# Score products of a two-map attention: full-array products of stacked hi and lo against products of 64 rows in two row tiles

## The chip, the cores and the metric

The kernel runs on one core of one Trainium2 chip. The metric is the device time of one execution in microseconds (us). Three timed runs of the kernel before took 1775.22, 1769.58 and 1770.94 us; the median is 1770.94 us.

## The reference, cut to what matters

The program is a two-layer backbone over 256 context tokens and 256 latent tokens of width 1024. Each layer normalises its input and feeds three mixers: a state-space scan (branch A), a differential attention (branch B) and a matrix-memory recurrence (branch C). Their outputs are gated, projected, merged and projected once more. Only branch B is touched here. It has 8 heads, each with two softmax maps over a head dimension of 64:

```python
def diff_attend(qb, k_all, v_all, lam):
    s = jnp.einsum('bqhcd,bkhcd->bhcqk', qb, k_all)       # c: the two maps, d: 64
    p = jax.nn.softmax(s, axis=-1)
    a = p[:, :, 0] - lam * p[:, :, 1]
    return jnp.einsum('bhqk,bkhe->bqhe', a, v_all)
```

Context queries see the 256 context keys; latent queries see all 512 keys. Layer 0 needs the outputs of all 512 tokens, layer 1 those of the 256 latent tokens alone.

## The kernel before, in words

There are four token tiles of 128 tokens (`NT` = 4): tiles 0 and 1 are context, 2 and 3 latent. `tq` holds the tiles whose outputs are needed, four in layer 0 and two (2 and 3) in layer 1. A quarter `qt` of the channels holds two heads; `qkv_proj(qt)` projects q, k and v of two heads in token layout, and `attn_prep(qt)` normalises and rotates q and k.

Products that must keep float32 accuracy are made of two operands in a reduced format (float32r): `hi`, the rounded value, and `lo`, the rest. A projection is then three products, hi x hi, hi x lo and lo x hi. They are the lines 149 to 151 (128 x 256 at a time) and 180 to 182 (mostly 128 x 512), and their weights are split on chip after each load (lines 119 to 121: ScalarE casts, VectorE subtracts).

`attn_tr(qt, h)` brings q and k of one head into channel layout with transposes on TensorE (lines 911 and 920): the 128 channels of a head are two maps of 64 rows each, in partitions 0 to 63 and 64 to 127. For each map it then builds, on 64 partitions at a time, one tile with hi of q in the map's own rows and lo of q in the other rows (lines 914 to 917), one tile with hi of k in both halves (lines 924 to 926; the second half is a copy made by GpSimd), and lo of k in the map's own rows (line 927).

`attn_head(qt, h)` goes over the token tiles `t` of `tq`. For each it makes the scores of both maps, 128 queries by N keys, with N = 256 for t < 2 and N = 512 otherwise. A map takes two matmuls: line 948 uses all 128 rows (hi x hi and lo x hi in one pass) and line 949 the 64 rows of the map (hi x lo). Each map has its own PSUM bank (`pe()`, three buffers). Then follow the row maximum (VectorE, line 951), the exponential (ScalarE, line 953), the difference of the two maps (VectorE, line 960), its transposes on TensorE (line 963), a copy (line 965) and the product with v (line 967). The group of four score matmuls of one tile `t` is called a set below. There are 48 sets: in layer 0, 8 heads with two sets of N = 256 and two of N = 512; in layer 1, 8 heads with two sets of N = 512.

The order on each engine is fixed when the program is built. A planner simulates the program and picks, for each engine, the ready instruction with the best priority; `band(0)` (loads, splits, evacuations) goes ahead of `band(1)` (the mixers), and that ahead of `band(2)` (projections). So projections that are due anyway (`fill`, lines 1025 to 1031, and those queued before) stand between the steps of the attention. After the attention comes branch C, in layer 0 together with `mod_block` (line 266), which computes modulation columns on VectorE, ScalarE and GpSimd.

Of the kernel before, what the change touches and what calls it, by code (L numbers as in the profile page):

```python
# [9 lines left out]
F32 = mybir.dt.float32  # L10
# [24 lines left out]
def hybrid_backbone_kernel(ctx: ExitStack, tc: tile.TileContext, A, out, dbg=None):  # L35
# [4 lines left out]
    # ---- priority bands: 0 loads, splits and evacuations; 1 mixers; 2 projections  # L40
# [52 lines left out]
    def bc(ap, n):  # L93
        """append a broadcast free dim of n"""
        return ap.unsqueeze(len(ap.shape)).to_broadcast(list(ap.shape) + [n])

    # ---- constants
# [20 lines left out]
    # ---- weight stream: granules of 4 k-tiles by 256 columns; hi/lo split on chip  # L118
# [4 lines left out]
    def granules(srcs):  # L123
        """srcs: dram pieces [1024, n] that make 256 columns; yields (k0, hi, lo)"""
        for g in range(2):
            with band(0):
                raw = mk(wts, [P, 4, 256], "raw", bufs=3)
                c = 0
                for src in srcs:
                    n = src.shape[1]  # L130
                    nc.sync.dma_start(
                        raw[:, :, c : c + n],
                        src[g * 512 : (g + 1) * 512, :].rearrange("(k p) n -> p k n", p=P),
                    )
                    c += n
                hi = mk(wts, [P, 4, 256], "whi", F32R, bufs=3)
                lo = mk(wts, [P, 4, 256], "wlo", F32R, bufs=3)
                split(raw, hi, lo)
            yield 4 * g, hi, lo

    def mm_tok(ps, lhs, tcol, k0, hi, lo):
        """one pair of token tiles times 4 k-tiles of weights; both tiles share a bank"""
        xh, xl = lhs
        for i in range(2):
            sl = slice(tcol + i * P, tcol + (i + 1) * P)
            o = ps[:, i * 256 : (i + 1) * 256]
            for j in range(4):
                k = k0 + j
                T.matmul(o, lhsT=xh[:, k, sl], rhs=hi[:, j, :], start=(k == 0 and i == 0), stop=False)  # L149
                T.matmul(o, lhsT=xh[:, k, sl], rhs=lo[:, j, :], start=False, stop=False)  # L150
                T.matmul(o, lhsT=xl[:, k, sl], rhs=hi[:, j, :], start=False, stop=(k == KT - 1 and i == 1))  # L151

    def proj_tok(srcs, lhs, pairs, evac):
        """out[tok, 256]; a pair of token tiles per bank, evacuated as [128, 2, 256]"""
        ps = {}
        with band(2):
            for p in pairs:
                ps[p] = pacc()
        for k0, hi, lo in granules(srcs):
            with band(2):  # L160
                for p in pairs:
                    mm_tok(ps[p], lhs, p * 256, k0, hi, lo)
        for p in pairs:
            with band(0):
                evac(p, ps[p].rearrange("p (t n) -> p t n", t=2))

    def proj_ch(srcs, lhs, ranges, evac, halves=False, gr=None):
        """out[128 channels, tokens] for 2 channel tiles; ranges[i] = (tok0, tok1)"""
# [34 lines left out]
    def rsqrt(src, n, scale, eps, pp=P, pool_=True):  # L203
        """1/sqrt(src*scale+eps) for a narrow [pp, n] tile"""
# [18 lines left out]
    # ---- modulation columns of one layer: four column tiles of the array share the contraction  # L223
    def mod_pair(l, cbs, pool, bufs, rbufs, between=None, each=None, end=False):
        with band(2):
            ps = pacc()
            for x, cb in enumerate(cbs):
                if x and between:
                    between()
                for k0 in range(0, KT, 2):  # L230
# [10 lines left out]
                    for j in range(2):  # L241
                        k = k0 + j
                        g = k % 4
                        # the second block's rows lie two below the first's
# [21 lines left out]
    def mod_block(l, cb, pool):  # L266
        """512 columns of the modulation: multiplied and added up by k-tile, TensorE sums the partitions"""
# [41 lines left out]
    # ---- narrow parameters of a layer: loads, and what is made of them  # L309
    def narrow(l, pool):  # L310
# [7 lines left out]
        gcs = mk(small, [P, 2, 2, 64], "gcs", bufs=1)  # (q|k), lat tile: cos * gain  # L318
        gsn = mk(small, [P, 2, 2, 64], "gsn", bufs=1)  # (q|k), lat tile: signed sin * swapped gain
# [16 lines left out]
        def compute():  # L336
            # scaled sign and decay columns
# [3 lines left out]
            # -lambda  # L341
# [5 lines left out]
            # rotary tables with the gains folded in; 1/sqrt(64) goes into q  # L347
# [11 lines left out]
    # ================= set-up  # L359
# [4 lines left out]
    with band(0):  # L364
# [11 lines left out]
        # small loads go between the large ones  # L376
        few = []
        for l in range(depth):
            w_ = prow[l]
            # per-channel parameters as rows: 16 for each layer  # L380
# [22 lines left out]
        # silu of the conditioning vectors, as columns  # L403
# [14 lines left out]
    def columns(l):  # L418
# [5 lines left out]
        # convolutions feed silu(x) = (x/2)(1 + tanh(x/2)): taps and bias are halved  # L424
# [8 lines left out]
    # the first weights, ahead of the second half of the modulation  # L433
# [17 lines left out]
    xcur = None  # x of the latent tiles after layer 0  # L451

    class Tokens:
        """token-layout [tokens, 1024] in slots of [128, 2 tiles, 512 columns]"""
# [4 lines left out]
        def __call__(self, b, p):  # L459
            """block of 256 columns of a pair of tiles: [128, 2, 256]"""  # L460
            return self.t[b // 2, p][:, :, (b % 2) * 256 : (b % 2 + 1) * 256]

        def tile(self, g, t):
            """half of the columns of one token tile: [128, 512]"""
            return self.t[g, t // 2][:, t % 2, :]

        def col(self, t, k):
            """[128 tokens, 128 channels]"""
            return self.tile(k // 4, t)[:, (k % 4) * P : (k % 4 + 1) * P]

    for l in range(depth):
        last = l == depth - 1
        w_in = A["w_in"][l]
        pq = (1,) if last else (0, 1)  # pairs of token tiles whose outputs are needed
# [13 lines left out]
        # ================= modulated norm -> hT (hi, lo)  # L488
# [63 lines left out]
        # ---------- pools of this layer  # L552
# [5 lines left out]
        sm = mk(mlrow, [P, 512], "sm", F32R)  # -M rows, hi over lo  # L558
        mlc = mk(mlrow, [P, 5, NT, 8], "mlc")  # w, sc, em, wk, cdec columns
        sa = mk(sp, [P, 512], "sa", F32R)  # L560
        col = mk(sp, [P, 5, NT, 2, 16], "col")  # -acs, exp(acs), dt*exp(end-acs), dt, exp(end)
# [19 lines left out]
        with band(1):  # L581
# [61 lines left out]
            # rows -> columns  # L643
# [8 lines left out]
            # per-chunk scalars on all partitions  # L652
# [32 lines left out]
        # ---------- depthwise convolution + silu of a channel tile (in PSUM) -> [128, n]  # L685
# [13 lines left out]
        # gate path: 2 silu(z) of [128, 2, 256]  # L699
# [7 lines left out]
        # ================= branch A: SSD  # L707
# [34 lines left out]
        def ssd_core(g):  # L742
            hs = slice(8 * g, 8 * g + 8)
            with band(1):
# [10 lines left out]
                # chunk states  # L755
# [70 lines left out]
        # ================= branch B: q, k, v of two heads  # L826
# [43 lines left out]
        # ================= branch B: differential attention  # L870
# [31 lines left out]
        halves_ = (slice(0, 64), slice(64, 128))  # the two maps of a head  # L902

        def attn_tr(qt, h):
            """q as hi over lo (map 1: lo over hi), k as hi over hi, and the lo of k"""
            res = qkv[qt][0]
            with band(1):
                q2, k2 = [], []
                pt = pm()
                for t in tq:  # L910
                    T.transpose(chunk(pt, t), res["q"][:, t, h * P : (h + 1) * P], ident)
                for m in range(2):
                    own, oth = halves_[m], halves_[1 - m]
                    x = mk(ap, [P, 512], f"q{m}", F32R, bufs=2)
                    S.copy(x[own, lo_:], pt[own, lo_:])
                    tt(x[oth, lo_:], pt[own, lo_:], x[own, lo_:].bitcast(F32), ALU.subtract)
                    q2.append(x)
                pt = pm()
                for t in range(NT):
                    T.transpose(chunk(pt, t), res["k"][:, t, h * P : (h + 1) * P], ident)  # L920
                kl = mk(ap, [P, 512], "kl", F32R, bufs=2)
                for m in range(2):
                    own, oth = halves_[m], halves_[1 - m]
                    x = mk(ap, [P, 512], f"k{m}", F32R, bufs=2)
                    S.copy(x[own], pt[own])
                    tsc(x[oth], x[own].bitcast(F32), 1.0, ALU.mult, 0.0, ALU.add, eng=G)
                    tt(kl[own], pt[own], x[own].bitcast(F32), ALU.subtract)
                    k2.append(x)
            aS[qt, h] = q2, k2, kl

        def attn_head(qt, h):
            vt = qkv[qt][0]["v"]
            ssB, r0B = aS[qt]
            q2, k2, kl = aS[qt, h]
            with band(1):
                po = pm()
                for t in tq:
# [8 lines left out]
                    for m in range(2):  # L946
                        o, own = es[m][0], halves_[m]
                        T.matmul(o, lhsT=q2[m][:, qs], rhs=k2[m][:, 0:N], start=True, stop=False)  # L948
                        T.matmul(o, lhsT=q2[m][own, qs], rhs=kl[own, 0:N], start=False, stop=True)  # L949
# [4 lines left out]
                    # E0 - lambda (sum0 / sum1) E1; the factor 1 / sum0 joins the norm below  # L954
# [20 lines left out]
        def attn_fin(qt):  # L975
            ssB, r0B = aS[qt]
            with band(1):
                # rms over a head: r0 / sqrt(mean((r0 o)^2) + eps)
# [19 lines left out]
        # ================= branch C: projections of one mLSTM head  # L998
# [49 lines left out]
        # branch A: rms over the row  # L1048
# [16 lines left out]
        # ================= branch C: mLSTM  # L1065
# [75 lines left out]
        def mo_post(j, ths):  # L1141
            with band(1):
# [8 lines left out]
                # zz holds 2 silu(z)  # L1151
# [74 lines left out]
        # ================= merge, in channel layout  # L1226
# [4 lines left out]
        per = D // nqt  # channel tiles in a slot of mixed  # L1231
        per = 2 if nqt == 512 else 4

        def transposed(y, scale_of):
            """token layout -> (hi, lo) [128, 8, tokens], scaled by a per-channel column"""
# [47 lines left out]
        # ================= output projection and residual  # L1283
        ep = tc.alloc_tile_pool(name=f"out{l}", bufs=1)
        xnew = Tokens(yx, "y", pq) if not last else xcur
        with band(1):
            gbc = {}
            for p in pq:
                gbc[p] = mk(ep, [P, D], "gbc", bufs=2)
                cc = 1 - p  # L1290
                for hf in range(2):
# [3 lines left out]
                    # half of the gate: the merge gates are 1 + tanh  # L1295
# [41 lines left out]
        # the other half of the columns: weights resident, one pair of token tiles after the other  # L1337
# [79 lines left out]
```

## Time and profile before

| What | Value |
|---|---|
| Median of three runs | 1770.94 us |
| Lowest and highest run | 1769.58 and 1775.22 us |
| Span of the profiled execution, first to last instruction | 1772.7 us |
| Time of the profiled execution outside of its span | not listed apart from the span |
| TensorE busy (matmul) | 1707.9 us, 96% |
| VectorE busy | 1233.4 us, 70% |
| ScalarE busy | 829.6 us, 47% |
| GpSimd busy | 296.4 us, 17% |
| DMA, mean over the span | 102 GB/s |

The busy time of a matmul in the profile runs from its start to a modelled end, and neighbours overlap; what a matmul occupies is read from the distance between the starts of two neighbours. Attention of layer 0 lies from about 280 to 560 us of the span, that of layer 1 from about 1317 to 1482 us. PE is TensorE's matmul row, PEld its weight load, DVE VectorE, ACT ScalarE, POOL GpSimd.

### The profile page before, as it was taken

To read this page: it belongs to the slowest core of one execution; us is meant where nothing else is said; L and a number is where in the kernel's file an instruction comes from. 1 tells how busy PE (TensorE), PEld (TensorE's weight loads), DVE (VectorE), ACT (ScalarE), POOL (GpSimd) and SP (SyncE) were. 2 spreads that over 40 slices of the span, in tenths; PEclk is the share of its full clock that TensorE was granted. 3 is DMA by queue.
4 is the path that set the end of the run, shared out by engine and by line. 5 is a ranking of instruction groups with operands and counts; after the bars stand their busy time and mean duration, and the time that the engine had idled before them with its cause. 6 is when DMAs were issued, how large, how long until landed. Compare 5 with 4: busy or idle time off the path is not lost.

```text
span 1772.7 us, 28884 instructions
## 1 busy us (share of the span) xinstructions
PE 1707.9 (96%) x11256; PEld 1512.4 (85%) x11256; DVE 1233.4 (70%) x2279; ACT 829.6 (47%) x1609; POOL 296.4 (17%) x296
## 2 busy tenths in 40 slices
PE   5999999999999798899999999999999999999998
PEld 1787889999899687888888889888898989999998
DVE  4798887777765999973434445787887876776565
ACT  3455535554545465642323333545554555444453
POOL 1012331111000646520011000111221210000000
PEclk8999999999999898999999999999999999999999
DMA  8422112222223434423323334232232223335554
GB/s 257 120 72 65 55 60 72 62 70 61 74 60 107 132 119 143 143 62 96 96 83 95 96 119 112 67 89 84 72 120 72 84 78 114 95 97 171 177 176 143
DMA packets 192052, 180.39 MB, mean 102 GB/s; under 512 B 20750, under 2 KB 178064, under 8 KB 191916
## 3 DMA queue, kind: packets, MB, share of 16 engines
q1 hardware_dynamic: 191916, 178.54, 33.5%
q8 instruction: 89, 1.46, 0.3%
q14 instruction: 47, 0.39, 0.1%
HBM read 177.47 MB, written 1.05 MB: 101 GB/s over the span
## 4 chain that ended last, share of the span: by engine, by line
PE 55%; DVE 6%; issue 1%; ACT 1%; POOL 0%; DVEq 0%; POOLq 0%; ACTq 0%
PE acc L180 9%; PE acc L182 9%; PE acc L181 9%; PE acc L151 6%; PE acc L149 6%; PE acc L150 6%; DVE macc L79 1%; PE pm L967 1%; PE pe L949 1%; DVE dn L82 1%; PE pm L1120 1%; DVE wlo L82 1%; PE pe L948 1%; PE pm L764 1%; PE pe L1104 1%
## 5 line engine op out<-in xcount | busy, mean ns | idle before, releaser
L82 DVE TENSOR_TENSOR wlo<-raw,whi 128x1024 fp32r<-128x1024 f32 x274 | 349.5, 1276 | 263.1 <-ACT whi L120 261.5
L149 PE MATMUL acc<-whi,hh 128*128 128x256 f32 x1728 | 504.9, 292 | 7.8 <-DVE modc L82 5.1
L151 PE MATMUL acc<-whi,hl 128*128 128x256 f32 x1728 | 506.5, 293 | 0.0
L150 PE MATMUL acc<-wlo,hh 128*128 128x256 f32 x1728 | 506.3, 293 | 0.0
L120 ACT CAST whi<-raw 128x1024 fp32r<-128x1024 f32 x274 | 287.7, 1051 | 372.2 <-PE acc L181 238.4
L149 PEld LDWEIGHTS acc<-whi,hh 128*128 128x128 f32 x1728 | 333.6, 193 | 17.4 <-issue 5.7
L151 PEld LDWEIGHTS acc<-whi,hl 128*128 128x128 f32 x1728 | 333.6, 193 | 10.7 <-issue 8.8
L150 PEld LDWEIGHTS acc<-wlo,hh 128*128 128x128 f32 x1728 | 333.6, 193 | 10.6 <-issue 8.1
L180 PE MATMUL acc<-hh,whi 128*128 128x512 f32 (+1 forms) x712 | 255.2, 361 | 2.5 <-DVE zz L79 2.5
L181 PE MATMUL acc<-hl,whi 128*128 128x512 f32 (+1 forms) x712 | 254.4, 358 | 0.2 <-DVE hl L82 0.2
L182 PE MATMUL acc<-hh,wlo 128*128 128x512 f32 (+1 forms) x712 | 253.3, 357 | 0.0
L180 PEld LDWEIGHTS acc<-hh,whi 128*128 128x128 f32 x712 | 134.4, 190 | 22.6 <-DVE zz L79 2.9
L181 PEld LDWEIGHTS acc<-hl,whi 128*128 128x128 f32 x712 | 135.0, 190 | 20.4 <-issue 3.1
L182 PEld LDWEIGHTS acc<-hh,wlo 128*128 128x128 f32 x712 | 135.0, 190 | 19.0 <-issue 1.2
L181 PE MATMUL acc<-yl,whi 128*128 128x512 f32 (+1 forms) x384 | 129.4, 339 | 0.0
L180 PE MATMUL acc<-yh,whi 128*128 128x512 f32 (+1 forms) x384 | 129.2, 339 | 0.0
L182 PE MATMUL acc<-yh,wlo 128*128 128x512 f32 (+1 forms) x384 | 128.9, 338 | 0.0
L82 POOL TENSOR_TENSOR macc<-macc,wm 128x512 f32<-128x512 f32 x56 | 81.3, 1452 | 116.6 <-ACT wm L290 106.4
L951 DVE TENSOR_REDUCE nmax<-pe 128x1 f32<-128x512 f32 (+1 forms) x96 | 56.3, 598 | 34.9 <-PE pe L949 33.7
L181 PEld LDWEIGHTS acc<-yl,whi 128*128 128x128 f32 x384 | 72.1, 188 | 8.5
L182 PEld LDWEIGHTS acc<-yh,wlo 128*128 128x128 f32 x384 | 71.9, 188 | 8.6
L180 PEld LDWEIGHTS acc<-yh,whi 128*128 128x128 f32 x384 | 72.0, 188 | 8.4
(310 smaller groups left out, 2848.8 us busy)
## 6 DMA issues: line engine op xcount, KB each, us to landing
raw<-in_w_in_dram SPq DMA_DIRECT2D x192, 512.0 KB
raw<-in_w_branch_dram SPq DMA_DIRECT2D x48, 512.0 KB
wm<-in_w_mod_dram SPq DMA_DIRECT2D x45, 512.0 KB
raw<-in_w_in_dram SPq DMA_DIRECT2D x48, 256.0 KB
raw<-in_w_out_dram SPq DMA_DIRECT2D x16, 512.0 KB
raw<-in_w_mod_dram SPq DMA_DIRECT2D x3, 512.0 KB
xin<-in_ctx_dram SPq DMA_DIRECT2D x2, 512.0 KB
xin<-in_x_dram SPq DMA_DIRECT2D x2, 512.0 KB
```

The costliest lines, as they stand in the source:

```text
L79: (eng or V).scalar_tensor_tensor(out=o, in0=a, scalar=s, in1=b, op0=op0, op1=op1)
L82: (eng or V).tensor_tensor(out=o, in0=a, in1=b, op=op)
L120: S.copy(hi, raw)
L149: T.matmul(o, lhsT=xh[:, k, sl], rhs=hi[:, j, :], start=(k == 0 and i == 0), stop=False)
L150: T.matmul(o, lhsT=xh[:, k, sl], rhs=lo[:, j, :], start=False, stop=False)
L151: T.matmul(o, lhsT=xl[:, k, sl], rhs=hi[:, j, :], start=False, stop=(k == KT - 1 and i == 1))
L180: T.matmul(o, lhsT=hi[:, j, cs], rhs=xh[:, k, a:b], start=(k == 0 and first), stop=False)
L181: T.matmul(o, lhsT=hi[:, j, cs], rhs=xl[:, k, a:b], start=False, stop=False)
L182: T.matmul(o, lhsT=lo[:, j, cs], rhs=xh[:, k, a:b], start=False, stop=(k == KT - 1 and final))
L764: T.matmul(pt, lhsT=BT[:, c, :], rhs=xw, start=True, stop=True)
L948: T.matmul(o, lhsT=q2[m][:, qs], rhs=k2[m][:, 0:N], start=True, stop=False)
L951: V.tensor_reduce(out=ng[:, m : m + 1], in_=es[m][0], axis=AX.X, op=ALU.max, negate=True)
```

## The change

`attn_tr` keeps q and k in their natural layout, both maps below each other in 128 partitions: one tile of hi and one of lo for q, and the same for k. Each is made by one ScalarE cast and one VectorE subtraction on 128 partitions. The tiles of swapped halves and the GpSimd copies go. `attn_head` makes the scores of a map by three matmuls of 64 rows (hi x hi, lo x hi, hi x lo); map 0 uses rows 0 to 63 of the array and map 1 rows 64 to 127, and the six matmuls of a set alternate between the two maps. The rest of the diff removes comments and docstrings.

```diff
         def attn_tr(qt, h):
             res = qkv[qt][0]
             with band(1):
-                q2, k2 = [], []
-                pt = pm()
-                for t in tq:
-                    T.transpose(chunk(pt, t), res["q"][:, t, h * P : (h + 1) * P], ident)
-                for m in range(2):
-                    own, oth = halves_[m], halves_[1 - m]
-                    x = mk(ap, [P, 512], f"q{m}", F32R, bufs=2)
-                    S.copy(x[own, lo_:], pt[own, lo_:])
-                    tt(x[oth, lo_:], pt[own, lo_:], x[own, lo_:].bitcast(F32), ALU.subtract)
-                    q2.append(x)
-                pt = pm()
-                for t in range(NT):
-                    T.transpose(chunk(pt, t), res["k"][:, t, h * P : (h + 1) * P], ident)
-                kl = mk(ap, [P, 512], "kl", F32R, bufs=2)
-                for m in range(2):
-                    own, oth = halves_[m], halves_[1 - m]
-                    x = mk(ap, [P, 512], f"k{m}", F32R, bufs=2)
-                    S.copy(x[own], pt[own])
-                    tsc(x[oth], x[own].bitcast(F32), 1.0, ALU.mult, 0.0, ALU.add, eng=G)
-                    tt(kl[own], pt[own], x[own].bitcast(F32), ALU.subtract)
-                    k2.append(x)
-            aS[qt, h] = q2, k2, kl
+                out = []
+                for nm_, ts, f0 in (("q", tq, lo_), ("k", range(NT), 0)):
+                    pt = pm()
+                    for t in ts:
+                        T.transpose(chunk(pt, t), res[nm_][:, t, h * P : (h + 1) * P], ident)
+                    xh = mk(ap, [P, 512], nm_ + "h", F32R, bufs=2)
+                    xl = mk(ap, [P, 512], nm_ + "l", F32R, bufs=2)
+                    S.copy(xh[:, f0:], pt[:, f0:])
+                    tt(xl[:, f0:], pt[:, f0:], xh[:, f0:].bitcast(F32), ALU.subtract)
+                    out += [xh, xl]
+            aS[qt, h] = out
...
-                    for m in range(2):
-                        o, own = es[m][0], halves_[m]
-                        T.matmul(o, lhsT=q2[m][:, qs], rhs=k2[m][:, 0:N], start=True, stop=False)
-                        T.matmul(o, lhsT=q2[m][own, qs], rhs=kl[own, 0:N], start=False, stop=True)
+                    for n, (x, y) in enumerate(((qh, kh), (ql, kh), (qh, kl))):
+                        for m in range(2):
+                            own = halves_[m]
+                            T.matmul(es[m][0], lhsT=x[own, qs], rhs=y[own, 0:N], start=(n == 0), stop=(n == 2))
```

## Rows read from the trace of the kernel before

**Rows 1.** The page: its first line, and TensorE's matmul row of part 1.

```profile
span 1772.7 us, 28884 instructions
...
PE 1707.9 (96%) x11256; PEld 1512.4 (85%) x11256; DVE 1233.4 (70%) x2279; ACT 829.6 (47%) x1609; POOL 296.4 (17%) x296
```

**Rows 2.** Stretches: length, busy us (instructions) by engine, PEclk, DMA share, GB/s.

```profile
280.00:560.00 280.00, 280.00 (x2014) 251.92 (x2013) 195.31 (x435) 143.10 (x312) 28.79 (x33) 1.00 0.23 66
1317.00:1482.00 165.00, 162.97 (x1142) 143.99 (x1142) 122.58 (x237) 90.27 (x175) 28.38 (x35) 0.98 0.27 79
...
575.00:765.00 190.00, 160.64 (x1015) 145.98 (x1014) 180.71 (x327) 106.66 (x209) 110.38 (x80) 0.92 0.43 130
...
1350.00:1360.00 10.00, 7.97 (x42) 6.44 (x42) 7.78 (x13) 4.86 (x10) 2.00 (x3) 0.74 0.36 105
```

**Rows 3.** PE in order of time (start, length, line), a set of N = 512.

```profile
489.77 0.60 PE L963 MATMUL pe<-ident,E 128*128 128x128 f32 x4
490.12 0.48 PE L948 MATMUL pe<-k,q 128*128 128x512 f32 x1
490.53 0.49 PE L949 MATMUL pe<-kl,q 64*128 64x512 f32 x1
...
491.39 0.50 PE L949 MATMUL pe<-kl,q 64*128 64x512 f32 x1
491.82 0.38 PE L151 MATMUL acc<-whi,hl 128*128 128x256 f32 x1
492.04 0.28 PE L149 MATMUL acc<-whi,hh 128*128 128x256 f32 x1
492.16 0.28 PE L150 MATMUL acc<-wlo,hh 128*128 128x256 f32 x1
```

**Rows 4.** PE in order of time, projection matmuls of 512 columns.

```profile
477.70 0.39 PE L182 MATMUL acc<-hh,wlo 128*128 128x512 f32 x1
...
479.96 0.39 PE L180 MATMUL acc<-hh,whi 128*128 128x512 f32 x1
```

**Rows 5.** PE in order of time, a set of N = 256.

```profile
292.54 0.36 PE L948 MATMUL pe<-k,q 128*128 128x256 f32 x1
292.83 0.38 PE L949 MATMUL pe<-kl,q 64*128 64x256 f32 x1
...
293.45 0.38 PE L949 MATMUL pe<-kl,q 64*128 64x256 f32 x1
293.76 0.38 PE L149 MATMUL acc<-whi,hh 128*128 128x256 f32 x1
293.99 0.28 PE L150 MATMUL acc<-wlo,hh 128*128 128x256 f32 x1
```

**Rows 6.** Line 948: matmuls, duration ns min/median/max, first and last start, forms.

```profile
L948 PE MATMUL pe<-k,q x96: 278/481/774, 281.5 to 1479.7; 128*128 128x512 f32 x64, 128*128 128x256 f32 x32
```

**Rows 7.** PE in order of time, modulation matmuls in column tiles of 32.

```profile
8.24 1.94 PE L245 MATMUL acc<-wm,cst 128*32 128x512 f32 x8 [0.26 <-ACT cst L411]
...
19.70 1.92 PE L245 MATMUL acc<-wm,cst 128*32 128x512 f32 x2 [5.93 <-DMA wm<-in_w_mod_dram]
```

**Rows 8.** PEld in order of time, weight loads of 16 rows by 128 columns.

```profile
58.56 0.82 PEld L421 LDWEIGHTS pm<-ident,prow 16*128 16x128 f32 x12 [0.35 <-ACT hf L91]
```

**Rows 9.** Groups by shape: line, engine, op, tiles, shapes | busy us, mean ns | idle before.

```profile
L88 POOL TENSOR_SCALAR k<-k 64x512 fp32r<-64x512 f32 x32 | 25.8, 808 | 140.7 <-ACT k L925 131.7 <-PE acc L150 9.0
...
L82 DVE TENSOR_TENSOR kl<-pm,k 64x512 fp32r<-64x512 f32 x32 | 22.0, 686 | 3.7 <-ACT k L925 3.1
L925 ACT CAST k<-pm 64x512 fp32r<-64x512 f32 x32 | 18.6, 580 | 8.9 <-PE pm L920 4.8 <-DVE kl L82 3.6
...
L82 DVE TENSOR_TENSOR p<-p,rt 128x512 f32<-128x512 f32 x16 | 10.9, 682 | 0.1
```

**Rows 10.** DVE in order of time, the map difference that line 963 transposes.

```profile
485.83 0.75 DVE L79 SCALAR_TENSOR_TENSOR E<-E,cf 128x512 f32<-128x512 f32 x1
```

**Rows 11.** PE in order of time, a score matmul that waited for GpSimd.

```profile
1355.30 0.77 PE L948 MATMUL pe<-k,q 128*128 128x512 f32 x1 [0.96 <-POOL k L88]
```

More of the change, by code (lines that the diff above doesn't have):

```diff
@@ L933, in attn_head @@
             ssB, r0B = aS[qt]
-            q2, k2, kl = aS[qt, h]
+            qh, ql, kh, kl = aS[qt, h]
             with band(1):
```

## The prediction

> **What bounds the kernel now.** I read the page first: TensorE's matmul row covers 96% of the span [rows 1]. That share alone proves little, since ends are modelled, so I went to the stretches. In the attention of layer 0 the busy matmul time equals the stretch (280.0 of 280 us) at clock 1.00, in layer 1 163.0 of 165 us; VectorE has 195 and 123 us there, ScalarE 143 and 90 us, DMA a share of about a quarter [rows 2]. So TensorE sets the pace where the change acts. Between 575 and 765 us the reader is to see the opposite: TensorE 160.6 of 190 us, VectorE 180.7 us [rows 2]; that stretch is VectorE's.
>
> Whether the attention is held by TensorE itself or by the chain of softmax steps behind each set is read from a wait. The map difference ends at 485.83 + 0.75 = 486.58 us [rows 10], and TensorE comes to its transposes at 489.77 us [rows 3]: they lay ready for 3.2 us. The time order shows projections without a pause around the sets. A TensorE that is some tenths of a us quicker per set finds its operands still waiting.
>
> **The change, step by step.** *What a set costs today.* Starts are compared, not lengths. Projection matmuls of 512 columns start 2.26 us apart over ten of them (477.70 to 479.96), 0.226 us each [rows 4]; of 256 columns 0.12 us (492.04 to 492.16) [rows 3]. The four score matmuls of N = 512 go from 490.12 to 491.82, 1.70 us, and the first projection behind them takes 0.22 us to the next instead of 0.12 [rows 3]. That makes 1.80 us, where four such matmuls in a dense stream would take 0.90. The excess sits at the changes between 128 and 64 rows: 0.41 - 0.226 = 0.18 us behind the first (490.12 to 490.53), 0.43 - 0.226 = 0.20 us behind the last (491.39 to 491.82), and 0.10 us on the first projection [rows 3]. A set has four such changes, since lines 948 and 949 alternate. For N = 256: 292.54 to 293.76 is 1.22 us, plus 0.23 - 0.12 = 0.11, so 1.33 us; the change costs 0.29 - 0.12 = 0.17 at the first and 0.31 - 0.12 = 0.19 at the last [rows 5].
>
> *What it will cost.* Six matmuls, all of 64 rows, so one change on entry and one on exit. The trace has no two row tiles at work together. The nearest row is that of column tiles: eight modulation matmuls on four tiles of 32 columns take 1.94 us, two on one tile 1.92 us [rows 7]. Independent tiles of the array thus run side by side at 0.01 us per extra tile; I take this for the row tiles and count three pairs. The trace also has weight loads of 128 columns for matmuls that stay in one 16-row tile: twelve in 0.82 us, at most 0.07 us each [rows 8], without the 0.2 us of a change. So a pair is worth the longer of one matmul and two loads: 0.226 us for N = 512, 0.14 us for N = 256. I add 0.07 us for the second map's first load.
> - N = 512: 0.18 + 3 x 0.226 + 0.20 + 0.10 + 0.07 = 1.23 us; 1.80 - 1.23 = 0.57 us saved.
> - N = 256: 0.17 + 3 x 0.14 + 0.19 + 0.11 + 0.07 = 0.96 us; 1.33 - 0.96 = 0.37 us saved.
>
> Line 948 has 64 matmuls of N = 512 and 32 of N = 256, two in a set [rows 6]: 32 and 16 sets. 32 x 0.57 + 16 x 0.37 = 18.2 + 5.9 = 24.1 us. With loads free and 0.01 us of stagger the sum is 32 x 0.63 + 16 x 0.49 = 28 us; with loads that can't run under a matmul of their own rows it is 15 us (a rival below). I take 24, as the column and 16-row tiles both show loads that don't hold up the stream.
>
> *The building of the operands.* For k of each of 16 heads one of two casts (580 ns) and one of two subtractions (686 ns) go, and both GpSimd copies (808 ns); for q likewise, a cast and a subtraction [rows 9]. The ones that stay work on 128 partitions instead of 64; a subtraction of 128 x 512 takes 682 ns against 686 for 64 x 512 [rows 9], so nothing is added. That frees some 20 us of VectorE, 17 of ScalarE and 26 of GpSimd, all in stretches that TensorE fills, and I count it as nothing; the cover is the projection matmuls, and if they ran out a set would save its share of the chain, some 1 to 2 us. One stall goes: at 1355.30 a score matmul waited 0.96 us for the GpSimd copy [rows 11], in a stretch where TensorE was busy 7.97 of 10 us at a mean clock of 0.74 [rows 2], that is about half the time at 1.2 instead of 2.4 GHz. The idle 2.0 us and the half of 5.2 us make 4.6 us lost there. The transposes and the difference before it were late too, so the next wait in line may keep most of it: 0 to 5 us, I take 0.
>
> *What is moved.* No DMA and no queue of SP or GpSimd gets a new instruction. The planner will make a new order, since the costs it plans with change. The price of one unlucky or lucky place is that of the stretch just named, so 5 us either way. Behind the attention of layer 0 VectorE's stretch begins; its loads follow the release of the attention's buffers, so it is shifted and keeps its length.
>
> *Sum.* 1772.7 - 24.1 = 1748.6 us of span. The span of the profiled execution lies 1.8 us above the median of the runs shown and within their scatter; against the median that is 1746.8, and I say 1747 us.
>
> **Rivals.**
> 1. *Own-row loads are exposed.* Each tile's second and third load waits for the matmul in its own rows. An exposed load is the 0.10 us that the first projection behind a set pays [rows 3], so two in a set add 0.20 x 48 = 9.6 us: 1757 us. Against it: the projections load weights at full rows and still follow each other at 0.12 us [rows 3]. The Trainium skill's page "TensorE: Matmul & The Clock Gate" (Part 3, "The mechanism") states that a weight load overlaps with a matmul in flight only where the row group differs, which would be this rival; the dense stream here disagrees for the full array, and no row shows it for 64 rows.
> 2. *The two row tiles don't overlap.* Six matmuls one behind the other, with two changes: 0.18 + 6 x 0.226 + 0.20 + 0.10 = 1.84 against 1.80 us, and 0.17 + 6 x 0.12 + 0.19 + 0.11 = 1.19 against 1.33 us. 32 x 0.04 - 16 x 0.14 = -1 us: 1770 us, no change. For it: overlap is shown for column tiles alone.
> 3. *Slower: each step between the row tiles costs what a step between 128 and 64 rows costs.* Then the set is six times 0.425 plus 0.10 = 2.65 us, and six times 0.307 plus 0.11 = 1.95 us: 32 x 0.85 + 16 x 0.62 = 37 us, 1808 us. It decides as soon as a score matmul of N = 512 holds the array over 1.7 / 6 = 0.28 us. For it: every change of rows that the trace shows is paid. Against it: stepping between column tiles costs nothing [rows 7]. The Trainium skill's page "TensorEngine Tiling (Array Packing)" (Tiling Modes, "Key Properties") puts the drain on a change of the tiling mode and not on a change of the tile, which speaks against this rival; the trace agrees for column tiles and has no row for row tiles.
>
> That the saving is found but lost again, because the softmax chain becomes late, has 3.2 us of slack against it and stands in the range only.
>
> **How the numbers follow.** Forecast 0.70 (own range 1737 to 1757: the 28 us, the 5 us of a lucky stall, and the 5 us of an unlucky order), rival 1 0.10, rival 2 0.09, rival 3 0.11. The range 1731 to 1768 holds the forecast with both lucky ends and rival 1, and leaves out rival 3 and most of rival 2: about 0.8. Within 0.3% is 5.3 us, about what a measurement of this kernel can tell from no change. Faster has the forecast and rival 1, less 0.01 for an order that eats the smaller saving: 0.79; same 0.10; slower 0.11.
>
> **What would show it.** In the trace after, the six score matmuls in order of time: the two of a pair start within 0.07 us, and pairs follow at about 0.23 us (N = 512) and 0.12 to 0.14 (N = 256); from the first start to the first projection about 1.1 us instead of 1.70. If pairs follow at 0.33, rival 1 holds; if single starts do at 0.226, rival 2; at 0.42, rival 3. TensorE should stay at 100% of the attention stretches, which become 16 x 0.57 + 16 x 0.37 = 15 us (layer 0) and 16 x 0.57 = 9 us (layer 1) shorter, and VectorE's stretch should keep its 190 us. The prediction is wrong if the sets shrink as said while a pause of TensorE in the attention or a longer stretch behind it takes the time back.

## The result, and the profile after

The changed kernel takes 1743.8 us (median of four runs, 1741.9 to 1748.7) against 1770.9 us before: 27 us less, ratio 0.9846 with a 95% interval of 0.9828 to 0.9864. The forecast was 1747 us. It was right; the steps below show which terms were off by some us, and a simpler change that gives more. One run of the experiment e3_full_rows took 2727 us at a mean granted clock of 0.56, and its figures below are of the other four.

The page after, the first line and TensorE's row [rows 1 before]:

```profile
span 1741.5 us, 28900 instructions
...
PE 1676.2 (96%) x11336; PEld 1497.6 (86%) x11352; DVE 1209.1 (69%) x2247; ACT 811.5 (47%) x1577; POOL 268.7 (15%) x264
```

TensorE's busy time fell by 31.7 us and its share stayed: it still sets the pace. The span is 1.75 us below the time of the same execution (1743.25 us). If the distance was the same before, that profiled execution took some 1774.5 us, 3.6 us over its median; so 31.2 us between the two spans and 27 us between the medians are one result.

Stretches after (length, busy us by engine, clock, DMA share, GB/s): attention of layer 0, VectorE's stretch behind it, attention of layer 1, and ten us of the latter [rows 2 before]:

```profile
281.00:541.00 260.00, 260.00 (x2053) 240.97 (x2052) 179.49 (x418) 131.81 (x293) 18.20 (x18) 1.00 0.25 70
...
561.00:750.00 189.00, 156.84 (x1019) 143.51 (x1024) 180.73 (x330) 106.03 (x207) 102.16 (x76) 0.93 0.44 129
...
1299.00:1447.00 148.00, 147.86 (x1144) 134.80 (x1143) 108.45 (x219) 79.31 (x158) 16.31 (x20) 1.00 0.30 82
...
1330.00:1340.00 10.00, 9.86 (x79) 8.77 (x79) 7.87 (x16) 7.42 (x17) 1.23 (x2) 1.00 0.48 140
```

TensorE is full in both attentions. VectorE's stretch kept its length (189 us, VectorE busy 180.7 as before) and only begins earlier. The last row answers to the pause near 1355 us [rows 2]: at the same place of layer 1 TensorE is busy 9.86 of 10 us, at clock 1.00 instead of 0.74.

TensorE in order of time (start, length), a set of N = 512 [rows 3 before]:

```profile
370.22 0.60 PE L952 MATMUL pe<-ident,E 128*128 128x128 f32 x4
370.75 0.50 PE L938 MATMUL pe<-kh,qh 64*128 64x512 f32 x2
371.09 0.39 PE L938 MATMUL pe<-kh,ql 64*128 64x512 f32 x2
371.32 0.40 PE L938 MATMUL pe<-kl,qh 64*128 64x512 f32 x2
371.64 0.39 PE L149 MATMUL acc<-whi,hh 128*128 128x256 f32 x1
371.87 0.28 PE L150 MATMUL acc<-wlo,hh 128*128 128x256 f32 x1
```

and one of N = 256 [rows 5 before]:

```profile
354.69 0.39 PE L938 MATMUL pe<-kh,qh 64*128 64x256 f32 x2
354.91 0.28 PE L938 MATMUL pe<-kh,ql 64*128 64x256 f32 x2
355.03 0.28 PE L938 MATMUL pe<-kl,qh 64*128 64x256 f32 x2
355.24 0.39 PE L150 MATMUL acc<-wlo,hh 128*128 128x256 f32 x1
355.46 0.28 PE L151 MATMUL acc<-whi,hl 128*128 128x256 f32 x1
```

Each row holds two matmuls, one in each row tile; in the records their starts are 3 to 4 ns apart. The row of a pair is hardly longer than the row of one matmul: 0.39 us for two (371.09), 0.39 us for one projection of 512 columns [rows 4]. Pairs follow at 0.34 us after the first (its load is exposed) and then at 0.23 us. From the first start to the first projection it is 0.89 us instead of 1.70, and 0.55 instead of 1.22.

The weight loads of the same set:

```profile
370.75 0.18 PEld L938 LDWEIGHTS pe<-kh,qh 64*128 64x128 f32 x2 [0.17 <-issue]
370.86 0.19 PEld L938 LDWEIGHTS pe<-kh,ql 64*128 64x128 f32 x2
371.09 0.19 PEld L938 LDWEIGHTS pe<-kl,qh 64*128 64x128 f32 x2
```

The loads pause for 0.17 us ahead of the first. In the matmul rows the change from 128 to 64 rows is seen twice: the four transposes ahead take 0.53 us up to the set (370.22 to 370.75), where four times their median distance of 0.11 us is 0.44, and the first pair takes 0.34 us instead of 0.23. The second and third load of each tile start while the matmul in the same rows runs.

The operands' building after, by shape [rows 9 before]: half as many instructions, on twice the partitions, of the same length.

```profile
L82 DVE TENSOR_TENSOR kl<-pm,kh 128x512 fp32r<-128x512 f32 x16 | 11.0, 686 | 7.5 <-ACT kh L915 7.5
...
L915 ACT CAST kh<-pm 128x512 fp32r<-128x512 f32 x16 | 9.4, 585 | 14.5 <-PE pm L912 14.5
```

### The profile page after: what moved, and what is told of

Read it like the earlier page. It is cut to its first block, busy times and chain, and to the rows that moved or that the text cites. A ratio compares the mean times of both kernels' runs of the same rounds, so it can differ in the third digit from the quotient of the medians.

```text
span 1741.5 us, 28900 instructions
## 1 busy us (share of the span) xinstructions
PE 1676.2 (96%) x11336; PEld 1497.6 (86%) x11352; DVE 1209.1 (69%) x2247; ACT 811.5 (47%) x1577; POOL 268.7 (15%) x264
## 4 chain that ended last, share of the span: by engine, by line
PE 55%; DVE 3%; issue 1%; ACT 1%; DMA 0%; POOL 0%; DVEq 0%; ACTq 0%
PE acc L180 9%; PE acc L182 9%; PE acc L181 9%; PE acc L150 6%; PE acc L149 6%; PE acc L151 6%; PE pe L938 1%; PE pm L956 1%; PE pm L1109 1%; PE pm L764 1%; PE pm L1088 1%; PE pe L1093 0%; PE pe L1230 0%; PE pm L1230 0%; DVE wlo L82 0%
## 5 line engine op out<-in xcount | busy, mean ns | idle before, releaser
L942 ACT ACTIVATE E<-pe,nmax 128x512 f32<-128x512 f32 (+1 forms) x96 | 58.6, 616 | 46.8 <-DVE nmax L940 46.7
```

Of the source, the lines that this page charges most:

```text
L942: S.activation(e_, o, AF.Exp, bias=ng[:, m : m + 1], accum_out=rs[:, m : m + 1])
```

## The experiments

The theory: side by side, two matmuls of 64 rows cost one; and each change between 128 and 64 rows costs about 0.2 us. The main rivals: the fewer changes did it all, or the lighter building of the operands did. "Sets" is summed over the time order of a whole trace: the distances from each score matmul to the next start, plus what the matmuls just ahead of and behind a set take over the median of their shape. A set is unbroken where no other matmul stands between its own.

| Kernel | Median, us | Ratio to before, 95% | Sets, us |
|---|---|---|---|
| before | 1771 to 1773 | 1 | 77.4 |
| after | 1743.8 | 0.983 to 0.986 | 49.9 |
| e5_one_row_tile | 1773.0 | 1.000 to 1.002 | 77.5 |
| e1_map_by_map | 1737.6 | 0.979 to 0.982 | 49.3 |
| e8_old_operands_two_changes | 1752.2 | 0.987 to 0.992 | 51.6 |
| e3_full_rows | 1738.5 | 0.979 to 0.983 | 37.9 |
| e6_full_rows_early_prep | 1729.5 | 0.975 to 0.977 | 37.4 |
| e9_tiles_early_prep | 1738.2 | 0.980 to 0.983 | 47.6 |
| e2_building_back | 1749.3 | 0.985 to 0.990 | 54.9 |
| e4_no_gpsimd | 1781.3 | 1.004 to 1.007 | 77.5 |
| e7_other_order | 1744.1 | 0.983 to 0.985 | 49.4 |

The same count for the unbroken sets alone, the median of each kind, shows both parts of the theory. Each row is, within 0.03 us, the matmul times that run one behind the other (0.23 and 0.12 us each) plus 0.2 us for every change of rows:

| Kernel | A set of N = 512, us | A set of N = 256, us | Matmul times | Changes |
|---|---|---|---|---|
| before | 1.71 | 1.25 | 4 | 4 |
| after | 1.09 | 0.74 | 3 | 2 |
| e5_one_row_tile | 1.78 | 1.10 | 6 | 2 |
| e8_old_operands_two_changes | 1.09 | 0.75 | 3 | 2 |
| e3_full_rows | 0.93 | 0.48 | 4 | 0 |

**e5: both maps in one row tile.**

```diff
-                            own = halves_[m]
+                            own = halves_[0]
                             T.matmul(es[m][0], lhsT=x[own, qs], rhs=y[own, 0:N], ...)
```

> The changed kernel with all six score matmuls of a set on rows 0 to 63: map 1's scores are left out, both maps are computed from map 0's rows. Counts, shapes and changes of tiling stay, only the second row tile goes. Theory (the two row tiles run side by side, and a step inside one tile is a dense one): a set has six matmul times instead of three, 3 x 0.226 us more for N = 512 and 3 x 0.116 us more for N = 256, so 32 x 0.68 + 16 x 0.35 = 27 us more than the changed kernel, about 1771 us, as the kernel before. Rival (the gain came from the fewer changes alone): 1744 us.

Measured 1773.0 us: all of the gain is gone. A set of its trace, TensorE in order of time:

```profile
297.18 0.74 PE L938 MATMUL pe<-kh,qh 64*128 64x512 f32 x2
297.76 0.63 PE L938 MATMUL pe<-kh,ql 64*128 64x512 f32 x2
298.23 0.62 PE L938 MATMUL pe<-kl,qh 64*128 64x512 f32 x2
298.78 0.38 PE L149 MATMUL acc<-whi,hh 128*128 128x256 f32 x1
```

The same counts, but two matmuls now fill 0.62 us, and a pair takes 0.47 us to the next instead of 0.23. The row tiles side by side are worth 28 to 29 us. The fewer changes alone are worth nothing here, because six matmuls of 64 rows replace four: the sum that rival 2 gave.

This run also tests the lighter building of the operands by itself, since it has that building while its sets cost what they cost before (77.5 us). Its attention of layer 1 has no pause either:

```profile
1317.00:1482.00 165.00, 164.88 (x1196) 149.33 (x1195) 112.54 (x226) 82.86 (x162) 16.30 (x20) 1.00 0.28 78
```

It still takes as long as the kernel before, so neither the building nor the lost pause shows as a gain of its own beyond the few us that another order of the planner is worth.

**e1: map by map.**

```diff
-                    for n, (x, y) in enumerate(((qh, kh), (ql, kh), (qh, kl))):
-                        for m in range(2):
+                    for m in range(2):
+                        for n, (x, y) in enumerate(((qh, kh), (ql, kh), (qh, kl))):
```

> The changed kernel with the six score matmuls of a set in another order: map 0's three, then map 1's three, so that a step to the other row tile comes once in a set and not five times. Theory (the two row tiles run side by side): only one pair overlaps, a set holds five matmul times instead of three, so 2 x 0.226 us more for N = 512 and 2 x 0.116 us more for N = 256: 32 x 0.45 + 16 x 0.23 = 18 us more than the changed kernel, about 1762 us. Rival (the gain came from the fewer changes between 128 and 64 rows alone): the number of those changes is the same, so 1744 us, no difference.

Both expectations missed: 1737.6 us, not slower but a little faster than the changed kernel. The trace, in order of time:

```profile
365.24 0.50 PE L938 MATMUL pe<-kh,qh 64*128 64x512 f32 x2
365.57 0.40 PE L938 MATMUL pe<-kh,ql 64*128 64x512 f32 x2
365.80 0.40 PE L938 MATMUL pe<-kl,qh 64*128 64x512 f32 x2
366.13 0.39 PE L149 MATMUL acc<-whi,hh 128*128 128x256 f32 x1
```

Program order as written is hi x hi, lo x hi, hi x lo of map 0 and then the three of map 1, but the starts come in pairs again: hi x hi of map 1 starts 10 ns behind hi x hi of map 0 and some 0.3 us ahead of map 0's second product. The records hold no program order, and the planner could have turned it, so that it stayed as written is inferred from the gaps in a pair: 3 to 4 ns in the changed kernel, where the two are neighbours in the program; 10 ns in the 43 unbroken sets here, where they are three apart; 6 to 7 ns in the five broken sets, where map 0's third product comes later and they are two apart. Read so, a matmul that waits for its own row tile doesn't hold up a later one in the other tile. The overlap stands; only my picture of one line of matmuls fell. The 6 us by which it beats the changed kernel are not in the sets (0.6 us); that they come from the planner's order is likely, but not shown.

**e8: the old operands, two changes instead of four.**

```diff
                     for m in range(2):
-                        o, own = es[m][0], halves_[m]
-                        T.matmul(o, lhsT=q2[m][:, qs], rhs=k2[m][:, 0:N], start=True, stop=False)
-                        T.matmul(o, lhsT=q2[m][own, qs], rhs=kl[own, 0:N], start=False, stop=True)
+                        T.matmul(es[m][0], lhsT=q2[m][:, qs], rhs=k2[m][:, 0:N], start=True, stop=False)
+                    for m in range(2):
+                        own = halves_[m]
+                        T.matmul(es[m][0], lhsT=q2[m][own, qs], rhs=kl[own, 0:N], start=False, stop=True)
```

> The kernel before with the four score matmuls of a set in another order: both of 128 rows first, then both of 64 rows, one in each row tile. The operands and their building stay as before. Theory (a change between 128 and 64 rows costs 0.2 us, row tiles run side by side): two changes and three matmul times as in the changed kernel, first start to first projection 0.226 + 0.41 + 0.43 = 1.07 us instead of 1.70 for N = 512 and 0.12 + 0.29 + 0.31 = 0.72 instead of 1.22 for N = 256: 32 x 0.63 + 16 x 0.50 = 28 us faster than before, 1743 us. Rival (the row tiles overlap only where both work on the natural operands, or a product of 64 rows behind one of 128 into the same bank waits): less than 15 us faster, over 1756 us.

```profile
306.40 0.71 PE L947 MATMUL pe<-k,q 128*128 128x512 f32 x2
307.04 0.50 PE L950 MATMUL pe<-kl,q 64*128 64x512 f32 x2
307.47 0.39 PE L150 MATMUL acc<-wlo,hh 128*128 128x256 f32 x1
```

A set takes 1.07 us from first start to first projection, exactly as summed, and the sets together 25.8 us less than before. The measured gain is 15 to 22 us, 1752.2 us: between the two expectations. Its runs scatter more than the others (1746.8 to 1759.5), and in the profiled one (1759.5) the first score comes at 288.2 us instead of 281.5, before anything that was edited. It also keeps a pause like the one near 1355 us of the kernel before (from 1340 to 1350 us TensorE is busy 7.23 of 10 us). The sets follow the theory; why the total lags by some us stays open.

**e3: no change of rows at all.**

```diff
-                        T.matmul(o, lhsT=q2[m][own, qs], rhs=kl[own, 0:N], start=False, stop=True)
+                        T.matmul(o, lhsT=q2[m][:, qs], rhs=kl[:, 0:N], start=False, stop=True)
```

> The kernel before with line 949 on all 128 rows: lhsT is the stacked q of hi and lo as in line 948, rhs is all of kl. The rows of the other map then add lo of q times lo of k of the other map, a product of two remainders. Theory (each change between 128 and 64 rows costs about 0.2 us): a set has four matmuls and no change, 0.90 us for N = 512 and 0.48 us for N = 256 where the kernel before has 1.80 and 1.33, so 32 x 0.90 + 16 x 0.85 = 42 us faster than before, about 1728 us, and 15 us faster than the changed kernel. Rival (only the work side by side counts; the 0.2 us are the price of a second product into the same bank): 1771 us, as before.

```profile
301.07 0.48 PE L948 MATMUL pe<-k,q 128*128 128x512 f32 x1
301.39 0.40 PE L949 MATMUL pe<-kl,q 128*128 128x512 f32 x1
301.62 0.40 PE L948 MATMUL pe<-k,q 128*128 128x512 f32 x1
301.86 0.39 PE L949 MATMUL pe<-kl,q 128*128 128x512 f32 x1
302.09 0.28 PE L151 MATMUL acc<-whi,hl 128*128 128x256 f32 x1
```

Four matmuls on the kernel before, in the same bank by twos, now follow each other at 0.23 to 0.24 us (0.32 behind the transposes) instead of 0.42 [rows 3]. The sets fell by 39.5 us, close to the 42 of the theory, and more than with the row tiles (27.5). The time fell by some 34 us, not 42: TensorE pauses elsewhere, above all here (PE in order of time, then the stretch):

```profile
1326.52 0.69 PE L920 MATMUL pm<-ident,p 128*128 128x128 f32 x2 [3.92 <-DVE p L82]
```

```profile
1320.00:1330.00 10.00, 5.41 (x31) 4.60 (x30) 7.38 (x15) 4.75 (x10) 3.29 (x4) 0.77 0.34 105
1330.00:1340.00 10.00, 10.00 (x74) 9.68 (x73) 6.35 (x16) 6.15 (x15) 2.98 (x5) 0.89 0.01 2
```

The transposes wait for the rotated k of the next two heads; 4.6 us are idle, and at mean clocks of 0.77 and 0.89 the array then ran 6.8 us at 1.2 instead of 2.4 GHz, which is up to 3.4 us more.

**e6 and e9: the preparation one head earlier**, on e3 and on the changed kernel.

```diff
         attn_tr(0, 0)
+        attn_prep(1)
...
-                if j % 2 == 0:
-                    attn_prep(j // 2)
+                if j % 2 and 1 < j < 7:
+                    attn_prep(j // 2 + 1)
```

> The kernel of e3 (all four matmuls on 128 rows) with attn_prep, which normalises and rotates q and k, issued one head earlier. Theory: the pause of 3.9 us near 1322 us in layer 1, where TensorE waits for that preparation, and the low clock behind it go: 4 to 6 us faster than e3, about 1734 us. Rival (another order of the planner, and another step late instead): 1739 us as e3, within 5 us either way.

> The changed kernel with attn_prep issued one head earlier, as in e6. Theory (the early preparation only takes away the pause in layer 1, and the changed kernel has none left there: TensorE is idle 0.14 us between 1330 and 1340 us at clock 1.00): no difference from the changed kernel, 1744 us, within 5 us for the planner's order; e6 is then 12 to 15 us ahead by its cheaper sets (0.90 against 1.17 us and 0.48 against 0.82 us). Rival (the early preparation is worth 10 us by the order that it gives): about 1734 us.

```profile
1292.00:1436.00 144.00, 144.00 (x1120) 138.95 (x1119) 117.55 (x235) 88.49 (x177) 28.89 (x33) 1.00 0.31 85
```

The stretch is layer 1's attention of e6: no pause, full clock. e6 takes 1729.5 us, 9 us less than e3 by the medians, and 8 when each is compared with the runs of the kernel before that were taken beside it. The pause and its low clock had been worth up to 8 by their rows, so I had priced it too low at 4 to 6; the planner's order changed as well, and its share is not shown apart. It is the fastest version, 40 to 45 us ahead of the kernel before. On the changed kernel, which has no such pause, the same edit gave 5.7 us, between its two expectations; 2.3 us of it lie in the sets, which now break less (50 unbroken groups of score matmuls instead of 55). e6 is 8.7 us ahead of it, where 12 to 15 were expected and the sets give 10.

**e2: the old building back.**

```diff
-                    S.copy(xh[:, f0:], pt[:, f0:])
-                    tt(xl[:, f0:], pt[:, f0:], xh[:, f0:].bitcast(F32), ALU.subtract)
-                    out += [xh, xl]
+                    xc = mk(ap, [P, 512], "kc", F32R, bufs=2) if nm_ == "k" else xh
+                    for own in halves_:
+                        S.copy(xh[own, f0:], pt[own, f0:])
+                        if nm_ == "k":
+                            tsc(xc[own], xh[own].bitcast(F32), 1.0, ALU.mult, 0.0, ALU.add, eng=G)
+                        tt(xl[own, f0:], pt[own, f0:], xh[own, f0:].bitcast(F32), ALU.subtract)
+                    out += [xc, xl]
```

> The changed kernel with the old amount of work for the operands: casts and subtractions on 64 partitions at a time, twice as many, and two GpSimd copies for each head through which hi of k must pass before the scores. Theory (all of the gain is TensorE's): no difference from 1744 us, within 5 us for another order of the planner. Rival (the shorter building of the operands gave the few us by which the gain exceeded the 24 us of the forecast): 3 to 5 us slower, 1747 to 1749 us, and a wait of TensorE for GpSimd in layer 1.

1749.3 us, 5.5 us slower by the medians; the intervals of the two ratios just overlap. The rival's number, but not its place: the profile shows no wait of TensorE for GpSimd in layer 1. The sets take 5.0 us more. They stand apart in 60 unbroken groups instead of 55, and each break pays two more changes; above all, 30 of the 288 score matmuls run without a partner, against 2 in the changed kernel, which is some 3 of the 5 us at 0.23 and 0.12 us for each lost pair. In order of time, three products of one map and then the first of the other:

```profile
1299.98 0.50 PE L942 MATMUL pe<-kc,qh 64*128 64x512 f32 x1
1300.32 0.39 PE L942 MATMUL pe<-kc,ql 64*128 64x512 f32 x1
...
1301.07 0.50 PE L942 MATMUL pe<-kl,qh 64*128 64x512 f32 x1
...
1303.44 0.49 PE L942 MATMUL pe<-kc,qh 64*128 64x512 f32 x1
```

The likely reason is that the operands of one map are ready later than those of the other, so that the planner puts other matmuls between and the side-by-side work of that set is lost. So the lighter building is worth up to 5 us, and it acts through the sets. With one order of the planner for each, this is an account of two traces and not a separate proof.

**e4: GpSimd's copies on ScalarE, in the kernel before.**

```diff
-                    tsc(x[oth], x[own].bitcast(F32), 1.0, ALU.mult, 0.0, ALU.add, eng=G)
+                    S.copy(x[oth], pt[own])
```

> The kernel before with the second half of hi of k cast by ScalarE from the transposes instead of copied by GpSimd. Theory (the stall of 0.96 us near 1355 us and the low clock behind it came from that copy): up to 5 us faster than before, 1766 to 1769 us. Rival (the next wait in line keeps it, or ScalarE's 19 us more cost as much): 1771 us, no difference.

Both missed: 1781.3 us, 8 us slower (6 to 12 by the interval), with the sets unchanged. In its trace a score matmul still waits as long as in the kernel before [rows 11], now for ScalarE's copy of the transposes (line 965):

```profile
1361.06 0.77 PE L948 MATMUL pe<-k,q 128*128 128x512 f32 x1 [0.96 <-ACT aT L965]
```

So the next wait in line kept it, and the GpSimd copy alone did not make the pause. The idle time of TensorE is 10 us more than before over the whole span. Whether ScalarE's 19 us of casts or the planner's order did that is not settled.

**e7: another order of the products** (hi x lo ahead of lo x hi).

```diff
-                    for n, (x, y) in enumerate(((qh, kh), (ql, kh), (qh, kl))):
+                    for n, (x, y) in enumerate(((qh, kh), (qh, kl), (ql, kh))):
```

> The changed kernel with the three products of a map in the order hi x hi, hi x lo, lo x hi. Each set costs the same on TensorE by every theory; lo of k is needed one step earlier, and the planner's order changes. It measures what an order of the planner is worth: 1744 us, and the distance from it is that worth, up to 6 us either way as between the changed kernel and e1.

1744.1 us: no difference from the changed kernel here. With e1 and e9, the same instructions in other orders gave 0, -6 and -6 us; that is about the worth of a planner's order here, close to the forecast's 5 us.

## Why the prediction was right, point by point

- *What bounds.* TensorE is full in both attentions after the change too, so what the sets saved (27.5 us) came out (27 us). The 3.2 us of slack held: TensorE is idle 0.14 us in the whole attention of layer 1, and never in that of layer 0.
- *The price of a set today* was a little too high: 1.80 and 1.33 us, where the table of sets has 1.71 and 1.25. The sum left out that the set's first matmul, which still has 128 rows, starts 0.08 us sooner behind the transposes than their median distance. The price of a change stands: 0.2 us each fits the sets with four, two and no changes.
- *The price of a set after* was too high as well. Predicted 1.23 and 0.96 us. Measured: 0.09 of entry ahead of the set + 0.89 + 0.10 on the next projection = 1.09 us after rounding, and 0.09 + 0.55 + 0.10 = 0.74 us. The sum charged 0.48 us for the two changes, which cost 0.4; this error and the one in today's price go the same way and nearly cancel in the difference, which is luck. The two terms that I had taken from the weight loads of 16 rows, 0.07 us of stagger and 0.14 us for a pair, were 0.004 and 0.12 us, and they make the 24 us too low. The forecast's own lower sum, with loads free, gave 28 us; the sets measured 27.5. Where I chose between the bounds, the column tiles were the nearer row for the loads too.
- *The place of the entry.* I said 1.1 us from first start to first projection; it is 0.89: half of the entry is paid ahead of the first start, half of the exit on the next projection, and there is no stagger.
- *The stall* near 1355 us was counted as 0 of a possible 0 to 5 us. After, no such pause is there. Its 4.6 us and the sets would give the 31 us between the spans, but that is not shown: TensorE's idle time over the whole span, summed between the matmul records, did not fall (52.7 us before, 53.3 after), and e5 lost the pause without becoming faster than the kernel before. What removed it is open too. The prediction put it down to the GpSimd copy, but e4 kept it without that copy, and e2 put copies of that kind back and did not bring it back.
- *Rival 1* (own-row loads exposed) is refuted by the loads that start under a running matmul, pairs at 0.23 us. The Trainium skill's page "TensorE: Matmul & The Clock Gate" (Part 3, "The mechanism") has a sentence that lets loads overlap only with matmuls of another row group; the trace disagrees for 64 rows as it did for 128. *Rival 2* (no overlap) is refuted by e5, which is that rival and takes its 1773 us. *Rival 3* (each step between tiles paid) is refuted by starts 3 to 4 ns apart.
- *The stretches.* First score to last product with v fell from 281.5-566.3 to 281.4-545.0 us in layer 0 (21 us, I said 15) and from 1317.6-1492.4 to 1299.1-1453.3 us in layer 1 (21 us, I said 9). About 10 us came back outside: the planner had moved projections behind the attention (2305 matmuls start from 1447 us on, against 2264 from 1483 us on before), which takes no time from the total but makes a stretch alone a poor measure of a saving.

## What to carry to other kernels

Compare starts, not lengths, around a change of tile shape: where matmuls of 128 and 64 rows alternate, each change cost about 0.2 us here, nearly as much as a matmul of 512 columns (0.23 us). Two row tiles halved the price of work with 64 rows, but before splitting, ask whether the small product can be filled up to full rows with something harmless: four full matmuls (e3) beat three pairs with their two changes. Then look for the pause that the faster engine now reaches; one preparation issued earlier was worth 8 to 9 us on top of e3.

## What the runs showed of the hardware that was not expected

- Matmuls of different row tiles need not start in program order: in e1 the first matmul of the second map, fourth in the program as written, starts 10 ns behind the first one, ahead of the second and third. The program order is inferred from the gaps, as said there. The Trainium skill's page "TensorE: Matmul & The Clock Gate" (Part 3, "The mechanism") has matmuls start in program order; this trace disagrees for starts in different row tiles.
- A pair of row tiles shares the array at full rate for 4-byte operands: 0.23 us for two matmuls of 64 x 512, 0.12 us for two of 64 x 256, against 0.47 us for two in one tile (e5).
- A change of rows costs 0.2 us in two parts of about 0.1 us, one on the matmul ahead of it and one on the matmul behind it. From 128 to 64 rows: 0.53 instead of 0.44 us for the four transposes, and 0.34 instead of 0.23 us for the first pair. From 64 to 128 rows: 0.32 instead of 0.23 us for the last pair, and 0.23 instead of 0.12 us for the first projection. Behind the transposes only the sum of the two parts is firm: in e3, without a change of rows, the first matmul there takes 0.32 us too, but starts 0.08 us sooner. A matmul between two changes pays both parts, as in the kernel before (0.43 instead of 0.23 us).
